# adaLN loads behind the boundary's weights, the time-step product in column groups, and decays from other queues, in a two-layer hybrid encoder on one core

## The chip, the core and the metric

One core of a Trainium2 chip runs the whole kernel. The metric is the device time of one execution in microseconds, lower is better, taken as the median of repeated runs. The engines are named as in the profile: PE is TensorE (matmuls), PEld its weight loads, DVE is VectorE, ACT is ScalarE, POOL is GpSimd and SP is SyncE, which only issues DMAs. ACT and POOL issue DMAs too. On chip data lie in SBUF (128 partitions); matmuls write to PSUM banks.

## The reference

One sequence of 512 tokens with 1024 features goes through two layers. The first mixes tokens with a gated short convolution, the second with a Mamba-2 state-space mixer; a SwiGLU feed-forward part follows each. Every part is wrapped in RMSNorms and in adaLN shift, scale and gate, which come from the conditioning vector `c`.

```python
mod = (jax.nn.silu(c) @ ada_w + ada_b).reshape(bsz, DEPTH, 2, 3, D_MODEL)
for i in range(DEPTH):
    shift, scale, gate = (mod[:, i, 0, k][:, None, :] for k in range(3))
    h = rmsnorm(x, norm_g[i, 0]) * (1.0 + scale) + shift
    y = short_conv_mixer(...) if i % 2 == 0 else ssd_mixer(...)
    x = x + gate * rmsnorm(y, norm_g[i, 1])
    shift, scale, gate = (mod[:, i, 1, k][:, None, :] for k in range(3))
    h = rmsnorm(x, norm_g[i, 2]) * (1.0 + scale) + shift
    y = swiglu_ffn(h, f_w_in[i], f_w_out[i])
    x = x + gate * rmsnorm(y, norm_g[i, 3])

def ssd_mixer(h, w_in, conv_w, conv_b, dt_bias, a_log, d_skip, norm_g, w_out):
    z, xbc, dt_raw = jnp.split(h @ w_in, [M_D_INNER, M_D_INNER + M_CONV_DIM], axis=-1)
    xbc = jax.nn.silu(causal_depthwise_conv(xbc, conv_w) + conv_b)
    xs, bm, cm = jnp.split(xbc, [M_D_INNER, M_D_INNER + g * n], axis=-1)
    dt = jax.nn.softplus(dt_raw + dt_bias)
    a = -jnp.exp(a_log)
    y = ssd_chunked(xs, dt, a, bm, cm) + d_skip * xs
    y = rms_normalize((y * jax.nn.silu(z)).reshape(..., groups)) * norm_g
    return y @ w_out
```

`ssd_chunked` sums `dt * a` along each chunk of 64 tokens (cs) and uses exp(cs) and differences of cs as decays. The columns of the state-space weight `m_w_in` are z (0 to 2047), xs (from `DIN` = 2048), B (from 2·`DIN`), C (from 2·`DIN`+`D`) and dt (32 columns from 6144).

## The kernel before

**Matmuls.** Activations lie feature-major, as `h[k]` tiles of 128 features by 512 tokens. Each float32 operand is split into a high part rounded to fp32r and a low part, and a product is three fp32r matmuls (high·high, high·low, low·high): `mm3`, which writes the lines L285, L286 and L287. One chunk of 128 output columns over K = 1024 is therefore 24 matmuls of 128x512. The split of a weight chunk (`split_w`, `load_w`) is a cast on ACT (L212 or L230) and a subtraction on DVE (L213 or L231).

**Order.** The programs of PE, ACT and DVE follow the order in which the code issues them in the blocks under `manual_schedule`; in the largest part of the kernel SP's and POOL's instructions are placed by a scheduler around that order. Each queue runs its instructions strictly one behind the other, so a waiting one holds up all that follow on that queue.

**Boundaries.** Between two parts stands a boundary: the last matmuls of one part, its norm and residual, the norm of the next part, the transposes of the result to feature-major (`tr`, xtr), the scale and shift (`u`), the split (`hi` on ACT, `lo` on DVE) and the first six weight chunks of the next part, the six leads (`k`, tile li). The table `BOUNDARY` in `out_begin` is that order, one step after the other; a step `name hf _ t` has a half of the tokens (0 or 1) and an index. The end of the table is

```python
hi1_2 hi1_3 lo1_2 k0_6 tr1_2 lo1_3 u1_4 hi1_4 u1_5 lo1_4 hi1_5 k0_7 tr1_3 lo1_5 u1_6 u1_7 hi1_6
hi1_7 lo1_6 k1_0 lo1_7 k1_1
```

The second half of tokens is finished in the leads only for K-tiles 0 and 1; tiles 2 to 7 (18 matmuls of 128x256 for each lead) follow as `rest(i)`. Hooks in `finish` run extra steps behind a named step.

**First boundary, into the first feed-forward part.** Its six leads come from `ffn_lead`; `after` loads the next weights (`more`, L221 on SP, two chunks, tile wst). adaLN's products for later parts run on DVE: rows of `ada_w` of 512 KB are loaded to staging tiles (`ada_load`, L1015, tile ada_st) and multiplied and added up (`ada_madd`, L127). `quarters` lists those still to be loaded. Each `ada_madd` frees a tile and issues the next load. Behind the boundary the feed-forward part computes sums of operand blocks and seven block products instead of eight (class `Units`: weights by `fetch`, with a sum that POOL's DMA adds up, L1241; class `Values`: sums of activations, L714 to L741; products sA, sB, sC, L665).

**Second boundary, into the state-space part.** `ssd_lead` lists the column ranges of the six leads: dt (32 columns padded with zeros to 128), two xs chunks, B, C, and the first z chunk of the first group of heads. The second z chunk is loaded by `load_w([(wm_in, P, P)])` as `more` and computed as a full chunk `pz` (`mm_chunk`, tile ip). The `u` values of the boundary lie in a rotating buffer of two.

**Opening of the state-space part.** `dt_steps` takes the raw dt (32 partitions, 512 tokens): transposes it to token-major (tokT, L1632), takes the softplus on DVE and ACT, builds the cumulative sums on PE (cumT, L1654), transposes them back (csh) and writes cs and exp(cs) to DRAM (cs_d, ecs_d, L1667 and L1669, from SP). `decays(g)` reads them back spread over all partitions (csb of 1 MB, two ecsb, L1677 and L1680, issued by ACT). `e_sub` (L1802), `e_exp` and `e_mul` turn csb into the decay matrices. `states` gives `prev`, which the product yo (L1825) reads. The convolutions of the four leads (`conv4`, tile cu) run between. `nxt` is the next group of heads; `nxt.weights(0)` loads its first weights (wst, L221) and `nxt.split(0)` casts the high part of the first chunk on ACT. `late_sums` continues adaLN's sums here (loads L1896); it also makes `four`, a 128x32 matrix on POOL that has a one in row p at column p mod 32.

## Time and profile before

| | us |
|---|---|
| median of 3 runs | 1322.79 (1322.65 to 1323.99) |
| profiled execution, its own time | 1323.32 |
| its span, first to last instruction | 1321.2 |
| PE busy | 1307.1 |
| DVE busy | 1023.3 |
| ACT busy | 724.7 |
| POOL busy | 109.9 |
| first boundary, its last steps and the start of the feed-forward part | about 223 to 265 |
| second boundary and opening of the state-space part | about 540 to 626 |

TensorE's mean granted clock is 0.998. All times inside the kernel are microseconds from the start of the span. In a row of the timeline the columns are start, duration, engine, line, operation, written tile<-read tiles, shapes and count; PE's matmuls are pipelined, so consecutive starts, not durations, give their cost. In a row of waits they are the waiting instruction, what it waited for, the total in us, how often, and the longest. "SPq" and "ACTq" rows are DMA issues.

### The profile page before, as it was taken

Reading aid. Unit: us, or ns where it says so; the run is one execution under the profiler, and the core shown is the slowest. Engines: PE = TensorE matmul, PEld = TensorE weight load, DVE = VectorE, ACT = ScalarE, POOL = GpSimd, SP = SyncE. Lnnn points to the kernel's source line nnn. Section 1 sums busy time; section 2 is a strip of 40 time slices with the busy share of each in tenths; the row PEclk is TensorE's granted clock in tenths of the full one; section 3 lists DMA queues with packets and bytes.
Section 4 is the critical chain, followed back from the end, with each engine's and each line's share of the span. In section 5 each row is a group of like instructions: output and inputs, shape, how many; then the busy total and the mean of one; then the engine's idle time right before and its main releaser. Section 6 shows DMA issues by size and latency. Waiting matters only on the chain.

```text
span 1321.2 us, 20459 instructions
## 1 busy us (share of the span) xinstructions
PE 1307.1 (99%) x7869; PEld 1149.2 (87%) x7869; DVE 1023.3 (77%) x1533; ACT 724.7 (55%) x1258; POOL 109.9 (8%) x135
## 2 busy tenths in 40 slices
PE   8999999999999999999999999999999999999998
PEld 7788889899998888898888888888789999998886
DVE  5577856978766987758998999977577777766888
ACT  5333345455533565656765667756574555544665
POOL 0000000111100240000000000000000111101330
PEclk9999999999999999999999999999999999999999
DMA  9767643789868983536764456523251888869871
GB/s 308 229 216 243 224 157 96 176 215 239 208 200 270 256 160 93 167 98 222 244 199 154 143 190 207 175 76 117 88 152 46 194 218 214 200 186 286 179 130 64
DMA packets 225429, 239.06 MB, mean 181 GB/s; under 512 B 10276, under 2 KB 177076, under 8 KB 224308
## 3 DMA queue, kind: packets, MB, share of 16 engines
q1 hardware_dynamic: 205008, 195.23, 47.7%
q0 software_dynamic: 16176, 29.63, 13.0%
q10 hardware_dynamic: 4148, 12.90, 3.0%
q8 instruction: 62, 1.02, 0.3%
q14 instruction: 35, 0.29, 0.1%
HBM read 203.76 MB, written 4.34 MB: 158 GB/s over the span
## 4 chain that ended last, share of the span: by engine, by line
PE 89%; DVE 4%; DMA 2%; ACT 2%; SPq 2%; issue 1%; DVEq 0%; ACTq 0%
PE sA L665 12%; PE ip L285 11%; PE ip L287 11%; PE ip L286 11%; PE y L387 8%; PE sC L665 6%; PE cA L2291 4%; PE sB L665 3%; PE cA L1322 3%; PE li L285 2%; PE li L287 2%; PE li L286 2%; PE li L947 1%; PE cD L2291 1%; PE cC L2291 1%; PE cB L2291 1%
## 5 line engine op out<-in xcount | busy, mean ns | idle before, releaser
L285 PE MATMUL ip<-h,whl 128*128 128x512 f32 x648 | 255.9, 395 | 0.2 <-DVE cv L1047 0.2
L287 PE MATMUL ip<-h,whl 128*128 128x512 f32 x648 | 252.4, 390 | 0.0
L286 PE MATMUL ip<-h,whl 128*128 128x512 f32 x648 | 252.3, 389 | 0.0
L285 PEld LDWEIGHTS ip<-h,whl 128*128 128x128 f32 x648 | 121.7, 188 | 26.2 <-issue 1.8
L287 PEld LDWEIGHTS ip<-h,whl 128*128 128x128 f32 x648 | 121.6, 188 | 25.8
L286 PEld LDWEIGHTS ip<-h,whl 128*128 128x128 f32 x648 | 121.8, 188 | 24.3
L665 PE MATMUL sA<-tq,whl 128*128 128x256 f32 x1008 | 131.2, 284 | 1.9 <-ACT g L675 1.9
L665 PEld LDWEIGHTS sA<-tq,whl 128*128 128x128 f32 x1008 | 125.8, 192 | 2.5 <-ACT g L675 2.1
L231 DVE TENSOR_TENSOR whl<-wst,whl 128x1024 fp32r<-128x1024 f32 x70 | 85.2, 1221 | 23.6 <-ACT whl L230 23.1
L127 DVE SCALAR_TENSOR_TENSOR ada_acc<-ada_st,csil,ada_acc 128x1024 f32<-128x1024 f32 x70 | 89.7, 1282 | 5.7 <-DMA ada_st<-in_ada_w_dram 4.3
L387 PE MATMUL y<-whlo,ys 128*128 128x512 f32 x384 | 89.6, 392 | 0.2 <-DVE ys L1936 0.2
L387 PEld LDWEIGHTS y<-whlo,ys 128*128 128x128 f32 x384 | 71.7, 188 | 16.4 <-issue 0.6
L285 PE MATMUL li<-h,whl 128*128 128x256 f32 x288 | 83.2, 289 | 0.0
L287 PE MATMUL li<-h,whl 128*128 128x256 f32 x288 | 81.5, 283 | 0.0
L286 PE MATMUL li<-h,whl 128*128 128x256 f32 x288 | 81.5, 283 | 0.0
L230 ACT CAST whl<-wst 128x1024 fp32r<-128x1024 f32 x70 | 72.7, 1040 | 2.2 <-DMA wst<-in_m_w_in_dram 2.2
L1241 POOL DMA_DIRECT2D sg<-sg x28 | 24.3, 870 | 535.5 <-DVE whl L213 230.0
L1690 DVE SCALAR_TENSOR_TENSOR cu<-ip,cols,cu 128x511 f32<-128x511 f32 (+2 forms) x84 | 62.8, 747 | 3.4 <-ACT cu L1687 1.4
L2291 PE MATMUL cA<-whlo,ao 128*128 128x512 f32 x264 | 61.0, 390 | 0.4 <-DVE c L2497 0.2
L2291 PEld LDWEIGHTS cA<-whlo,ao 128*128 128x128 f32 x264 | 49.3, 188 | 11.5 <-ACT whlo L2256 1.2
L285 PEld LDWEIGHTS li<-h,whl 128*128 128x128 f32 x288 | 55.2, 192 | 0.0
L286 PEld LDWEIGHTS li<-h,whl 128*128 128x128 f32 x288 | 55.2, 192 | 0.0
(383 smaller groups left out, 2680.7 us busy)
## 6 DMA issues: line engine op xcount, KB each, us to landing
ada_st<-in_ada_w_dram SPq DMA_DIRECT2D x96, 512.0 KB, 5.3
wsu<-in_f_w_in_dram SPq DMA_DIRECT2D x30, 512.0 KB, 5.8
sg<-in_f_w_in_dram SPq DMA_DIRECT2D x56, 256.0 KB, 3.4
wsu<-in_f_w_in_dram SPq DMA_DIRECT2D x56, 256.0 KB, 4.9
wst<-in_m_w_in_dram SPq DMA_DIRECT2D x14, 1024.0 KB, 5.3
wst<-in_f_w_in_dram SPq DMA_DIRECT2D x10, 1024.0 KB, 6.2
wst<-in_m_w_in_dram SPq DMA_DIRECT2D x20, 512.0 KB, 5.4
wst<-in_a_w_in_dram SPq DMA_DIRECT2D x9, 1024.0 KB, 7.1
```

The costliest lines, as they stand in the source:

```text
L127: dve.scalar_tensor_tensor(acc, w, csil[:, k:k + 1], acc, MUL, ADD)
L230: later.append((lambda sw=sw, w=w: act.copy(w[:, 0, :nk, :], sw), lambda sw=sw, w=w: dve.tensor_tensor(w[:, 1, :nk, :], sw, w[:, 0, :nk, : ...
L231: lambda sw=sw, w=w: dve.tensor_tensor(w[:, 1, :nk, :], sw, w[:, 0, :nk, :].bitcast(F32), SUB)))
L285: pe.matmul(dst, w_at(w, 0, kk), a[:, 0, sl], start=start, stop=False)
L286: pe.matmul(dst, w_at(w, 0, kk), a[:, 1, sl], start=False, stop=False)
L287: pe.matmul(dst, w_at(w, 1, kk), a[:, 0, sl], start=False, stop=stop)
L387: pe.matmul(pst, a[:, al, tk], wt[:, wl, kk, :], start=k == 0 and i == 0, stop=k == K - 1 and i == 2, skip_group_check=bool(held))
L665: pe.matmul(dst, w[:, wl, k0 + k, :], self.moving(q, k, al), skip_group_check=True, start=q in self.FIRST and k == 0 and i == 0, stop=k == ...
L1241: pool.dma_start(dst, src, accum_op=ADD)
L1322: pe.matmul(bank[r, sub], a[:, al, q, tk], w[:, wl, q, :], start=first and k == 0, stop=False, skip_group_check=True)
L1690: dve.scalar_tensor_tensor(u[:, sft:], pst[:, :T - sft], w[3 - sft], u[:, sft:], MUL, ADD)
L2291: pe.matmul(bank[r][sub], a[:, al, q, tk], w[:, hl, q, :], start=first and k == 0, stop=last and k == 2, skip_group_check=True)
```

## The change

It has four parts. The diff, cut to its core:

```diff
@@ first boundary @@
             madds = ada_begin(3)
+            put_off, quarters[:] = quarters[:], []
             begun = out_finish(parts, tail, ws0, {"lo0_7": (madds, madds), "lo1_3": (madds,)})
+            quarters[:] = put_off
...
             vs = Values(h, tq, va, [raw[1][:, 2 * b:2 * b + 2, :] for b in range(2)])
             lo_, hi_ = HALVES
+            for _ in range(3):
+                ada_load()
             part_of.fetch(0)
@@ second boundary @@
     ssd_lead = [lambda later, srcs=srcs: load_lead([(wm_in, c0, n) for c0, n in srcs], tile4l, later)
-                    for srcs in (((6144, NH), (DIN, P)), ((DIN + P, P), (2 * DIN, P)),
-                                 ((2 * DIN + D, P), (0, P)))]
+                    for srcs in (((DIN, P), (DIN + P, P)), ((2 * DIN, P), (2 * DIN + D, P)), ((0, P), (P, P)))]
...
             def u_(self, hi, j):
-                u = self.u[hi, j] = tmp.tile([P, 256], F32, tag="uh", name="u", bufs=2)
+                if values:
+                    u = self.u[hi, j] = values[j][:, HALVES[hi]]
+                else:
+                    u = self.u[hi, j] = tmp.tile([P, 256], F32, tag="uh", name="u", bufs=2)
...
-                               lambda: load_w([(wm_in, P, P)]), ys=ys, held=held)[2]
+                               lambda: None, ys=ys, held=held, values=values)[2]
...
-            begun = finish(tail_w, leads)
-        h, lead_ps, rest, wz1 = begun
+            va = wst_p.tile([P, 4, T], F32, tag="wst", name="va")
+            vb = [ao_p[0].tile([P, 2, T], F32, tag="ao", name="vb") for _ in range(2)]
+            values += [va[:, j, :] for j in range(4)] + [vb[j // 2][:, j % 2, :] for j in range(4)]
+            wdt = flat2(ao_p[0].tile([P, 2, T], F32, tag="ao", name="wdt"))[:, :KD * NH]
+            wdt = wdt.rearrange("p (k n) -> p k n", n=NH)
+            dma(wdt, wm_in[:, 6144:6144 + NH].rearrange("(k p) f -> p k f", p=P))
+
+            def dt_product():
+                pd = aux_ps("dtp")
+                for k in range(KD):
+                    g = k % 4 * NH
+                    pe.matmul(pd[g:g + NH, :], wdt[:, k, :], values[k], start=k < 4, stop=k >= 4,
+                              tile_position=(0, g), skip_group_check=True)
+                raw = t2("raw")
+                act.activation(raw, pd, AF.Identity, bias=dtb)
+                raws.append(raw)
+                yield
+
+            raws = []
+            begun = finish(tail_w, leads, {"lo1_7": (dt_product(),)})
+        h, lead_ps, rest, _ = begun
@@ dt_steps, decays @@
             for cc in range(NCH):
-                pe.transpose(pt[:, cc * NH:(cc + 1) * NH], raw[:, cc * P:(cc + 1) * P], ident[:NH, :NH])
+                pe.matmul(pt[:, cc * NH:(cc + 1) * NH], raw[:, cc * P:(cc + 1) * P], four[:, 0:NH],
+                          start=True, stop=True)
...
-            dma(cs_d.rearrange("h (c t) -> (h c) t", t=P), cs_hm)
+            dma_s(cs_d.rearrange("h (c t) -> (h c) t", t=P), cs_hm)
             act.activation(ecs_hm, cs_hm, AF.Exp)
-            dma(ecs_d.rearrange("h (c t) -> (h c) t", t=P), ecs_hm)
+            dma_s(ecs_d.rearrange("h (c t) -> (h c) t", t=P), ecs_hm)
...
-        def decays(g):
+        def decays(g, put=dma_s):
@@ opening @@
             nxt.weights(0)
...
-            convs = [cur.conv(i, lead_ps[1 + i]) for i in range(4)]
+            convs = [cur.conv(i, lead_ps[i]) for i in range(4)]
+            dts = dt_steps(raws[0])
+            next(dts)
             rest(0)
-            raw = dt_raw(lead_ps[0])
-            rest(1)
-            dts = dt_steps(raw)
-            next(dts)
             nxt.split(0)
...
-            rest(5)
             next(dts)
-            pz = mm_ps("ip")
-            mm_chunk(pz, wz1[0], h, ks=range(0, 2))
+            rest(4, range(2, 6))
             next(dts)
-            cur.e, cur.ecs = decays(0)
+            rest(4, range(6, KD))
+            cur.e, cur.ecs = decays(0, pool.dma_start)
...
-            mm_chunk(pz, wz1[0], h, ks=range(2, KD))
+            rest(5)
```

**adaLN's loads.** `quarters` is emptied while the first boundary is built, so no `ada_madd` in it issues the next load; three loads are issued after it, before `fetch(0)`. SP's queue, where ada_st are adaLN's loads, wst the weights `more` that follow the boundary's leads, and sg and wsu the first `fetch`. Before:

```order
L263 DMA wst<-in_f_w_in_dram 128x8x256
L1015 DMA ada_st<-in_ada_w_dram 128x1024 x6
L221 DMA wst<-in_f_w_in_dram 128x8x256
L604 DMA sg<-in_f_w_in_dram 128x4x128
L605 DMA sg<-in_f_w_in_dram 128x4x128
L608 DMA wsu<-in_f_w_in_dram 128x8x128
```

and now:

```order
L264 DMA wst<-in_f_w_in_dram 128x8x256
L1019 DMA ada_st<-in_ada_w_dram 128x1024 x3
L222 DMA wst<-in_f_w_in_dram 128x8x256
L1019 DMA ada_st<-in_ada_w_dram 128x1024 x3
L1652 DMA ea<-in_m_a_log_dram 128x32
L608 DMA sg<-in_f_w_in_dram 128x4x128
L609 DMA sg<-in_f_w_in_dram 128x4x128
L612 DMA wsu<-in_f_w_in_dram 128x8x128
```

Three of the six adaLN loads now stand behind the weights, and the small load of `m_a_log` (ea), which stood in the opening of the state-space part, stands here, ahead of the first fetch.

**dt.** The six leads are now the four convolution chunks and both z chunks. The padded lead, the memset of its pad, the separate load and split of the second z chunk and the chunk `pz` are gone. The boundary keeps its `u` values whole, in a weight buffer (va) and two others (vb). Behind step lo1_7, ahead of k1_1, eight float32 products of these values with the 32 dt columns (wdt) go into four column groups of one PSUM bank, two for each group. ACT adds the bias (dtb, now 128 rows, zero from row 32 on) and copies the four groups to raw (128x512); tokT is now a product with `four`, which adds up the groups and transposes at once. `four` is made earlier, after the first boundary, not in `late_sums`. The next group's first projection (`project(0)`) takes a bank of the other PSUM pool.

**The cast of the next group's weights.** The first cast of `nxt.split(0)` moves on ACT into the second boundary. There va and vb are the kept values, u before. Before:

```order
L522 CAST h_5076<-u 128x256
L519 ACTIVATE u<-xtr,mods,acol 128x256
L522 CAST h_5077<-u 128x256
L455 ACTIVATE ss<-ss 128x1
L519 ACTIVATE u<-xtr,mods,acol 128x256
```

and now:

```order
L526 CAST h_5081<-va 128x256
L523 ACTIVATE vb<-xtr,mods,acol 128x256
L231 CAST whl<-wst 128x1024
L526 CAST h_5082<-vb 128x256
L456 ACTIVATE ss<-ss 128x1
L523 ACTIVATE vb<-xtr,mods,acol 128x256
```

The cast (L231) stands between the value and the high part of feature tile 4. Its load (`nxt.weights(0)`) stands on SP behind wdt, two writes of x_d and one adaLN load; before, it was ahead of them all.

**The decays.** On ACT's queue in the opening, before:

```order
L1659 ACTIVATE dte_tok<-dte_tok 128x128
L1660 ACTIVATE dec<-cumT 128x128
L1668 ACTIVATE csb<-csb 128x128
L1677 DMA csb<-cs_d 128x2048
L1680 DMA ecsb<-ecs_d 64x2x512 x2
L1692 ACT_TABLE_LOAD
```

and now:

```order
L1683 ACTIVATE dte_tok<-dte_tok 128x128
L1684 ACTIVATE dec<-cumT 128x128
L1691 DMA cs_d<-csb 128x128
L1692 ACTIVATE csb<-csb 128x128
L1693 DMA ecs_d<-csb 128x128
L1716 ACT_TABLE_LOAD
```

The two writes come to ACT from SP, and the three reads of the first group go from ACT to POOL's queue; those of the later groups stay on ACT.

More of the change, by code (lines that the diff above doesn't have):

```diff
@@ L90, in trunk_kernel @@
     mcw = cols3
-    dtb = consts.tile([NH, 1], F32, name="dtb")
+    dtb = consts.tile([P, 1], F32, name="dtb")
+    pool.memset(dtb, 0.0)
     dcol = consts.tile([P, 16], F32, name="dcol")
@@ L372, in trunk_kernel, with out_begin @@
     LATE = 3
-    def out_begin(s, w, get_act, K, gg, xn_tile, first, lead, after, stage=None, ys=None, held=None):
+    def out_begin(s, w, get_act, K, gg, xn_tile, first, lead, after, stage=None, ys=None, held=None, values=()):
         ys = [None, None] if ys is None else ys
@@ L536, in k, with rest @@
                             kk == 0, kk == KD - 1)
-            def rest(self, i):
-                for kk in range(2, KD):
+            def rest(self, i, ks=range(2, KD)):
+                for kk in ks:
                     mm3(self.acc[i][:, HALVES[1]], self.ws[i], kk, self.h[kk], HALVES[1], False, kk == KD - 1)
@@ L1616, in st1 @@
             return sp.tile(list(shape), F32, name=name, tag=name, bufs=bufs)
-        def dt_raw(psd):
-            raw = t2("raw")[:NH, :]
-            act.activation(raw, psd[:NH, :], AF.Identity, bias=dtb)
-            return raw
         def dt_steps(raw):
@@ L1882, in norm @@
                     dve.scalar_tensor_tensor(y, y, mng[:, 2 * g + q:2 * g + q + 1], self.rg, MUL, MUL)
+        uh = tmp.tile([P, 256], F32, tag="uh", name="four", bufs=2)
+        four = uh[:, 0:P]
+        make_four(four)
         def late_sums():
-            uh = tmp.tile([P, 256], F32, tag="uh", name="four", bufs=2)
             sets, st = (64, 72, 80, 88), []
@@ L1900, in late_sums @@
                 load(n)
-            yield uh[:, 0:P]
+            yield
             for i, q0 in enumerate(sets):
@@ L1965, in trunk_kernel @@
             next(convs[0])
-            rest(2)
+            rest(1)
             next(convs[1])
@@ L1970, in trunk_kernel @@
             nxt.later[1][1]()
+            rest(2)
+            next(convs[2])
             rest(3)
-            next(convs[2])
-            rest(4)
             next(convs[3])
-            rest(5)
             next(dts)
-            pz = mm_ps("ip")
-            mm_chunk(pz, wz1[0], h, ks=range(0, 2))
+            rest(4, range(2, 6))
             next(dts)
-            cur.e, cur.ecs = decays(0)
+            rest(4, range(6, KD))
+            cur.e, cur.ecs = decays(0, pool.dma_start)
             for i in range(3):
@@ L1984, in trunk_kernel @@
             steps_late = late_sums()
-            four = next(steps_late)
-            make_four(four)
-            mm_chunk(pz, wz1[0], h, ks=range(2, KD))
+            next(steps_late)
+            rest(5)
             next(convs[3])
@@ L1990, in trunk_kernel @@
                 next(convs[i])
-            cur.project_z(0, lead_ps[5])
-            cur.project_z(1, pz)
+            for q in range(2):
+                cur.project_z(q, lead_ps[4 + q])
             nxt.later[2][0]()
```

15 lines of the change are left out of this document (9 added, 6 removed).

## The prediction

> **What bounds the kernel now.** I read the busy shares first, then what TensorE (PE) waits for, then the chain of waits at the two places that the change touches.
>
> ```profile
> PE 1307.1 (99%) x7869; PEld 1149.2 (87%) x7869; DVE 1023.3 (77%) x1533; ACT 724.7 (55%) x1258; POOL 109.9 (8%) x135
> PE sA L665 <- ACT g L675: 1.9, 1, 1.9
> PE sC L665 <- DVE raw L1209: 0.2, 1, 0.2
> ```
>
> PE is busy in 1307.1 of 1321.2 us, and its longest wait once the loads have begun to come is 1.9 us. So the kernel is a queue of matmuls without holes. Only two things shorten it: fewer matmuls, or one of these small waits gone. Work taken from ScalarE (ACT), VectorE (DVE) or a DMA queue counts only if a PE wait hangs on it. Where 1.9 us comes from, the chain shows (start, us, what):
>
> ```profile
> 223.50 7.27 DMA wst<-in_f_w_in_dram
> 230.79 1.06 ACT whl L212
> 231.87 2.37 DVE whl L213 x2
> 237.94 1.29 DVE ada_acc L127
> 259.56 0.28 ACT g L675
> 259.88 2.15 PE sA L665 x12
> ```
>
> It starts at a weight load that lands late, and 36 us of DVE and ACT work run behind it almost without a gap to the matmul that waits.
>
> **Part 1, the adaLN loads held back.** SyncE's queue (SP) and ACT at that place (on the ACT rows, the idle time before them in brackets):
>
> ```profile
> 181.94 41.51 SPq L1015 DMA_DIRECT2D ada_st<-in_ada_w_dram  x5
> 223.50 0.43 SPq L221 DMA_DIRECT2D wst<-in_f_w_in_dram  x1
> 225.11 0.38 SPq L604 DMA_DIRECT2D sg<-in_f_w_in_dram  x1
> 225.77 0.86 ACT L522 CAST h<-u 128x256 fp32r<-128x256 f32 x2 [1.26 <-DVE u L517]
> 230.79 2.00 ACT L212 CAST whl<-wst 128x1024 fp32r<-128x1024 f32 x2 [4.16 <-DMA wst<-in_f_w_in_dram]
> sg<-in_f_w_in_dram SPq DMA_DIRECT2D x56, 256.0 KB, 3.4
> ```
>
> The load of wst stands behind adaLN loads that each wait until DVE has used a staging buffer, so it is issued at 223.50. In the changed order three of those loads come behind it, and it can go out at about 189, when the three ahead of it have been issued. Then ACT casts as soon as its own work ends, at 226.63 (225.77 + 0.86), not at 230.79: the head of the chain starts 4.16 us earlier. PE needs 1.9 + 0.2 us of that (the waits at sA and sC), so 2.1 is the most; PE itself cannot run ahead. I take **-2.0**. The ends are 0 (another input becomes the last) and -2.1. What is late next: the first fetch (sg, then the accumulating DMA on POOL). The load of m_a_log now stands ahead of it on SP and waits for the boundary's last DVE step, so sg goes out some 2.4 us after 225.11, at about 227.5. With 3.4 us to landing (the median of the sg loads) that is 231, and what is read from it, the sum on POOL and then split_y, comes only after the DVE steps on the values. The three held-back loads then feed the first sums(2), which is at 237.94 in the old chain; their data are of 512 KB and are issued before the wsu. If they land last, DVE stops there and the gain goes: that is a rival below.
>
> **Part 2, dt.** Removed: one chunk of 24 matmuls 128x512 (pz, the second z chunk, now among the six leads in place of the padded dt lead). Two rows of PE 24 matmuls apart give its price:
>
> ```profile
> 599.02 0.39 PE L285 MATMUL ip<-h,whl 128*128 128x512 f32 x1
> 604.46 0.39 PE L285 MATMUL ip<-h,whl 128*128 128x512 f32 x1
> 18.76 0.39 PE L947 MATMUL li<-h,whl_b 128*128 128x512 f32 x1
> 19.08 1.08 PE L194 MATMUL ada_pe<-ada_st,rows 128*32 128x128 f32 x32
> 20.09 0.96 PE L947 MATMUL li<-h,whl_b 128*128 128x512 f32 x3
> 926.01 1.10 PE L1868 MATMUL ssg<-accg,ones 128*128 128x512 f32 x2
> ```
>
> 604.46 - 599.02 = 5.44 us, or 0.227 each: **-5.44**. Added: dtp, eight float32 products of 32 columns over 512, k-th into column group k mod 4. The kernel has the same form already, with 128 columns in motion: ada_pe, 16 products shown as 32 passes, in 1.08 us. From 18.76 to 20.09 is 1.33, less 0.23 for the li matmul itself leaves 1.10, and the three li behind it take 0.96 where three pipelined ones take 0.39 + 2 x 0.23 = 0.85: in all about 1.2 us. One float32 pass of 512 costs about 0.45 by ssg (two passes in 1.10, less the 0.17 by which a 0.39 matmul outlasts its pitch), so one of 128 about 0.11; 32 of them in a row would be 3.6. Hence four run at once: eight slots, 0.87, and 0.35 for going into the tiled form and out. For dtp: 16 passes, four at once, 4 x 0.45 = 1.8, plus 0.35 is 2.15; with 0.43 a pass and the switch half hidden it is 1.9. I take **+2.0**. All in a row it would be 16 x 0.45 = 7.2, the other bound.
>
> tokT goes from transposes to float32 products, eight passes for four. The rows, with the pitch of the 128x256 matmuls ahead of it:
>
> ```profile
> 583.55 0.28 PE L286 MATMUL li<-h,whl 128*128 128x256 f32 x1
> 583.67 0.28 PE L287 MATMUL li<-h,whl 128*128 128x256 f32 x1
> 583.88 0.43 PE L1632 MATMUL tokT<-ident,raw 32*128 32x32 f32 x4
> 584.24 0.39 PE L285 MATMUL li<-h,whl 128*128 128x256 f32 x1
> 592.97 0.39 PE L1654 MATMUL cumT<-ea,mask 128*128 128x128 f32 x2
> ```
>
> Four passes take 0.36 (584.24 - 583.88), so four more are **+0.3** (0.1 to 0.4). Part 2 is -5.44 + 2.0 + 0.3 = **-3.1** (-3.5 to -2.6). The memset, the load and the split of one weight chunk that also go (a CAST of 1.0, a subtraction of 1.2) lie on ACT and DVE under running matmuls: nothing. The memset of dtb adds 0.1 at the start on POOL, and PE's first matmul needs only what stands ahead of it: nothing, at most 0.1.
>
> Does the dt chain still arrive? Its end on DVE:
>
> ```profile
> 591.68 0.29 DVE L1650 SCALAR_TENSOR_TENSOR ea<-dt_tok,ea 128x128 f32<-128x128 f32 x1
> ```
>
> It ends at 591.97 with ea, and cumT on PE, which reads it, follows 1.0 later at 592.97. In the changed order tokT has 36 matmuls of 128x256 (two of the six rest passes, 36 x 0.12 = 4.3 us) less ahead of it and dtp more: 2.3 earlier, at 581.6. cumT too loses 36 and gains dtp and the longer tokT: 2.0 earlier, at 591.0. The slack stays at about 1 us; nothing is added. dtp's own inputs are there: the last value is written by DVE just ahead of the last 18 matmuls, as before, and wdt (128 KB) is loaded ahead of the adaLN load of 552.44 (below), over 20 us before.
>
> **Part 3, the decays.** On the queues now:
>
> ```profile
> 595.43 0.34 SPq L1667 DMA_DIRECT2D cs_d<-csb  x1
> 598.74 0.36 ACTq L1677 DMA_DIRECT2D csb<-cs_d  x1
> 600.58 1.28 ACT L1692 ACT_TABLE_LOAD   x1 [4.84 <-DVE cu L1690]
> 607.48 2.46 ACT L1802 ACTIVATE csb<-csb,cs_tok 128x128 f32<-128x128 f32 x8
> DMA to landing us min/median/max: 5.0/6.3/7.5
> 620.46 0.42 DVE L1793 TENSOR_TENSOR prev<-prev,st 128x256 f32<-128x256 f32 x1
> 624.24 1.50 PE L1825 MATMUL yo<-ct,prev 128*128 128x128 f32 x12
> ```
>
> The two writes take 0.8 us of ACT's queue, inside its 4.84 us of idling. The csb load (1 MB), which waits 3.3 us for the write, goes out 2.0 us earlier, like cumT, at 596.7, now on POOL, and e_sub(0) wants it at about 604.4 (607.48 less part 2's 3.1). Issued like POOL's other transfers (0.86 us a piece) and landing as the csb loads did (5.0 to 7.5 after the issue), it is there at 602.6 to 605.1: 0 to 0.7 us of waiting on ACT. PE notices only through prev, which ends 3.4 us before yo (624.24 - 620.88): nothing, up to 3.4 us of lateness.
>
> By the Trainium skill, "DMA: Bandwidth & Descriptors", SWDGE vs HWDGE, the queue of POOL builds its descriptors in SBUF state from which a busy DVE can lock it out, which speaks against this move; DVE is busy in those 10 us. The page's own fit for such a transfer, 2.0 us plus the bytes at 436 GB/s, makes 4.4 us of 1 MB, an estimate by which nothing is late.
>
> **Part 4, a cast that moves.** At the second boundary the high part of the next group's weights now stands in ACT's order between u0_4 and hi0_4, and its load on SP stands behind x_d and an adaLN load:
>
> ```profile
> 552.44 1.34 SPq L1896 DMA_DIRECT2D ada_st<-in_ada_w_dram  x2
> 558.71 0.56 ACT L519 ACTIVATE u<-xtr,mods,acol 128x256 f32<-128x256 f32 x1
> 564.25 1.34 ACT L499 ACTIVATE xn<-x,ss 128x512 f32<-128x512 f32 x2
> 566.95 0.60 PE L508 MATMUL xtr<-ident,xn 128*128 128x128 f32 x4
> wst<-in_m_w_in_dram SPq DMA_DIRECT2D x14, 1024.0 KB, 5.3
> ```
>
> Issued at about 552.8 and 5.3 us on the way (the median), it lands at 558.1, before ACT gets there at 559.3. Everything behind it on ACT (hi0_4, the squares, the root, xn) is then 1.0 later; xn ends at 566.6 at worst, not 565.59, and PE's transpose of it is at 566.95: hidden, with 0.4 left. It costs from a landing after 559.7 on, us for us; I count 0 (to +1).
>
> **Sum.** -2.0 - 3.1 = -5.1 against the profiled execution: its span of 1321.2 plus the 2.1 around it are 1323.3, which becomes 1318.2. The median of the runs lies 0.5 below the profiled one (1322.8 for 1323.3), so I say **1317.7**; its own range is 1316.4 to 1319.3.
>
> **Rivals.**
> (a) *The gain at the first boundary only moves.* Another input is last there: the held-back adaLN loads at sums(2), or sg. For it: DVE runs without a gap from 231.87 on, so any late input is passed on. Against: these loads are out before 231. Then part 2 remains: -3.1, 1319.7. 11%.
> (b) *The column groups do not overlap at 512 columns.* Then dtp is 7.2 + 0.35, part 2 is +2.4, the whole +0.4: 1323.2. Only the ada_pe row, with 128 columns, speaks against it. 6%.
> (c) *Slower: the csb load drags on POOL's queue.* If that queue moves bytes in proportion to its 256 KB sums, which land after 4.8 us in the median,
>
> ```profile
> DMA to landing us min/median/max: 3.3/4.8/10.8
> ```
>
> 1 MB takes 19.2 us from the end of its issue (597.6) and lands at 616.8; wanted at 604.4, it is 12.4 late, and 3.4 of that is hidden ahead of yo: +9.0, less 5.1, is +3.9: 1326.7. It decides from a landing after 607.8 on, and makes the kernel slower by more than 0.2% from 615.6 on. Against: those sums also read their target back and take an engine's addition, and the DMA engines are the same for all queues. 8%.
> (d) *The cast blocks the second boundary.* A landing of 7 us or more, x_d and two adaLN loads being in flight: PE waits 1 to 2 at xtr: 1319.2. 5%.
>
> **How the numbers follow.** Forecast 70%, (a) 11, (b) 6, (c) 8, (d) 5. The range 1315.8 to 1320.8 takes in the forecast's own range with the runs' spread of 0.6 below, (a) and (d), and leaves out (b) and (c), some 16%, with a little at the lower end. 0.2%, 2.65 us, is about what can be told from no change: faster means under 1320.1. Faster: 69 of the forecast's 70, 8 of (a), 4 of (d): 81%. Within: (b), the rest of (a) and (d) and 1: 11%. Slower: (c), 8%.
>
> **What would show it.** Right: PE's list of waits without sA from g; wst issued near 189; 16 passes of dtp in about 2 us; 24 fewer L285 to L287 rows of 128x512; no PE wait for xtr above 0.5 us at the second boundary; csb landed within 8 us of POOL's issue and no PE wait at yo. Wrong: DVE idle for ada_st behind the fours of the first boundary (a), dtp of 7 us (b), ACT idle before e_sub(0) above 3.4 us (c), ACT idle before the moved cast (d). A gain above 5.6 would mean that something ran earlier which I do not see.

## The result, and the profile after

The changed kernel takes 1317.76 us (median of 6, 1316.24 to 1319.07) against 1323.04 us before (median of 6); the ratio is 0.9958, 95% interval [0.9945, 0.9971]. That is 5.3 us faster, 5.1 was forecast, and 1317.7 as the time. Its profiled execution has a span of 1316.1 us. One execution, in experiment 12, took 1432.84 us at a granted clock of 0.85; the ratios leave it out, and the median given there, 1316.79, is 1316.69 without it. The sum came out right with terms off in opposite directions, so that it fits this closely is in part luck, and most of what follows is about those terms.

Busy shares and PE's longer waits after the change, behind the start of the kernel (waiting instruction, what for, us in total, times, longest):

```profile
PE 1301.8 (99%) x7865; PEld 1142.9 (87%) x7865; DVE 1020.2 (78%) x1531; ACT 723.4 (55%) x1257; POOL 113.2 (9%) x139
PE xtr L509 <- ACT xn L500: 1.1, 3, 0.6
PE ggp L320 <- DVE gcol L159: 0.8, 1, 0.8
PE yo L1851 <- DVE prev L1819: 0.2, 1, 0.2
```

PE is busy 5.3 us less, and sA from g is gone from the list. The wait at ggp lies in the convolution layer, where nothing was changed; a second profile of the same kernel (below) does not have it. The spans of its six executions lie between 1314.0 and 1316.1 us, so steps are read here as the shift of single matmuls between neighbouring places, not as differences of spans.

At the first boundary, SP and ACT after the change:

```profile
182.62 5.87 SPq L1019 DMA_DIRECT2D ada_st<-in_ada_w_dram  x2
188.54 0.43 SPq L222 DMA_DIRECT2D wst<-in_f_w_in_dram  x1
217.16 6.96 SPq L1019 DMA_DIRECT2D ada_st<-in_ada_w_dram  x3
228.17 0.43 SPq L608 DMA_DIRECT2D sg<-in_f_w_in_dram  x1
227.21 1.99 ACT L213 CAST whl<-wst 128x1024 fp32r<-128x1024 f32 x2
```

The weights go out at 188.5 (189 was said), ACT casts them without waiting, and sg goes out at 228.2; neither PE nor DVE waits for it.

In the opening of the state-space part, dtp and tokT on PE with the matmuls around them, and the first decays on POOL and ACT:

```profile
573.91 0.28 PE L288 MATMUL li<-h,whl 128*128 128x256 f32 x1
574.12 1.06 PE L1614 MATMUL dtp<-va,wdt 128*32 128x512 f32 x8
575.01 1.04 PE L1614 MATMUL dtp<-vb,wdt 128*32 128x512 f32 x8
575.98 0.39 PE L286 MATMUL li<-h,whl 128*128 128x256 f32 x1
578.23 0.98 PE L1655 MATMUL tokT<-four,raw 128*128 128x32 f32 x8
579.04 0.36 PE L286 MATMUL li<-h,whl 128*128 128x256 f32 x1
```

```profile
594.12 0.56 POOL L1701 DMA_DIRECT2D csb<-cs_d  x1 [109.44 <-DVE cu L1714]
603.96 2.45 ACT L1828 ACTIVATE csb<-csb,cs_tok 128x128 f32<-128x128 f32 x8 [3.02 <-DMA csb<-cs_d]
```

From the last li before dtp to the first behind it are 2.07 us; one pitch of 0.12 is that matmul's own, so dtp costs 1.95, and 0.1 more shows at the next li. tokT takes 0.81, before 0.36. The csb read lands 9.8 us after its issue, and ACT stands 3.0 us for it.

At the second boundary, the moved cast on ACT and, on PE, the four transposes that follow it by way of xn, with the first li behind them:

```profile
556.91 1.05 ACT L231 CAST whl<-wst 128x1024 fp32r<-128x1024 f32 x1 [1.20 <-DMA wst<-in_m_w_in_dram]
563.39 0.87 PE L509 MATMUL xtr<-ident,xn 128*128 128x128 f32 x4
564.02 0.36 PE L286 MATMUL li<-h,whl 128*128 128x256 f32 x1
```

The weights of the cast went out at 549.65 and landed after 7.2 us, where 5.3 was taken. ACT stood 1.2 us for them, xn came later by that and the cast, and the transposes with the step to the next li take 0.63 us, 0.35 before (566.95 to 567.30). These 0.3 us are not among PE's waits: the one that waits is PEld, for the weights of a transpose (PEld for xn, 0.3).

The next table gives the starts of six matmuls in us, the shift against the kernel before in brackets. Rows: sC just ahead of the wait at the first boundary, the first full sA product behind it, the first li behind a transpose of the second boundary, the first xtok of the opening, the first yd of the second group of heads, the first transpose of the third boundary. "Again" is a second profile of the changed kernel, "reads on ACT" an experiment below.

| matmul | before | after | again | reads on ACT |
|---|---|---|---|---|
| sC | 254.93 | 255.28 (+0.35) | 254.27 (-0.66) | 254.23 (-0.70) |
| sA | 264.35 | 261.04 (-3.31) | 260.03 (-4.32) | 259.99 (-4.36) |
| li | 567.30 | 564.02 (-3.28) | 563.68 (-3.62) | 563.09 (-4.21) |
| xtok | 609.90 | 603.54 (-6.36) | 603.19 (-6.71) | 602.59 (-7.31) |
| yd | 665.68 | 659.97 (-5.71) | 659.94 (-5.74) | 658.36 (-7.32) |
| xtr | 975.17 | 969.91 (-5.26) | 969.18 (-5.99) | 967.60 (-7.57) |

So the first boundary gives 3.66 us in both profiles (0.35 + 3.31, 4.32 - 0.66). Counted from the product ahead of sC, so that the wait at sC is in it as in the forecast's 2.0, it is 3.99 in both (sA starts at 253.17 before, 253.85 and 252.84 after): twice the forecast. The opening from li to xtok gives 3.08 and 3.09; 3.1 was forecast. Between xtok and the second group's yd 0.65 and 0.97 are lost again; nothing was forecast there.

### The profile page after: what moved, and what is told of

Same layout as the page of the kernel before. It is cut to its first block, busy times and chain, and to the rows that moved or that the text cites. A ratio compares the mean times of both kernels' runs of the same rounds, so it can differ in the third digit from the quotient of the medians.

```text
span 1316.1 us, 20444 instructions
## 1 busy us (share of the span) xinstructions
PE 1301.8 (99%) x7865; PEld 1142.9 (87%) x7865; DVE 1020.2 (78%) x1531; ACT 723.4 (55%) x1257; POOL 113.2 (9%) x139
## 4 chain that ended last, share of the span: by engine, by line
PE 83%; DVE 7%; DMA 4%; ACT 3%; SPq 2%; issue 1%; ACTq 0%; DVEq 0%; POOLq 0%
PE sA L669 12%; PE y L388 8%; PE ip L286 8%; PE ip L288 8%; PE ip L287 8%; PE sC L669 6%; PE cA L2316 4%; PE cA L1327 3%; PE sB L669 3%; PE li L286 2%; PE li L288 2%; PE li L287 2%; DMA ada_st<-in_ada_w_dram 2%; PE li L951 1%; DVE ada_acc L128 1%
## 5 line engine op out<-in xcount | busy, mean ns | idle before, releaser
L286 PE MATMUL ip<-h,whl 128*128 128x512 f32 x640 | 252.6, 395 | 0.2 <-DVE cv L1051 0.2
L288 PE MATMUL ip<-h,whl 128*128 128x512 f32 x640 | 249.3, 390 | 0.0
L287 PE MATMUL ip<-h,whl 128*128 128x512 f32 x640 | 249.2, 389 | 0.0
L286 PEld LDWEIGHTS ip<-h,whl 128*128 128x128 f32 x640 | 120.2, 188 | 25.8 <-issue 1.8
L288 PEld LDWEIGHTS ip<-h,whl 128*128 128x128 f32 x640 | 120.1, 188 | 25.5
L287 PEld LDWEIGHTS ip<-h,whl 128*128 128x128 f32 x640 | 120.2, 188 | 24.0
L231 ACT CAST whl<-wst 128x1024 fp32r<-128x1024 f32 x70 | 72.7, 1040 | 1.8 <-DMA wst<-in_m_w_in_dram 1.8
L286 PEld LDWEIGHTS li<-h,whl 128*128 128x128 f32 x288 | 55.2, 192 | 0.8 <-issue 0.8
L287 PEld LDWEIGHTS li<-h,whl 128*128 128x128 f32 x288 | 55.2, 192 | 0.0
L288 PEld LDWEIGHTS li<-h,whl 128*128 128x128 f32 x288 | 55.1, 191 | 0.0
```

Source lines behind the costliest of these rows:

```text
L231: later.append((lambda sw=sw, w=w: act.copy(w[:, 0, :nk, :], sw), lambda sw=sw, w=w: dve.tensor_tensor(w[:, 1, :nk, :], sw, w[:, 0, :nk, : ...
L286: pe.matmul(dst, w_at(w, 0, kk), a[:, 0, sl], start=start, stop=False)
L287: pe.matmul(dst, w_at(w, 0, kk), a[:, 1, sl], start=False, stop=False)
L288: pe.matmul(dst, w_at(w, 1, kk), a[:, 0, sl], start=False, stop=stop)
```

## Experiments

All times of a group were taken beside the kernel before on the same chip: 1322.84 for experiments 1, 2, 3 and 5, 1322.58 for 6 to 9, 1322.85 for 4, 10, 11 and 12.

**1. The hold-back alone.** The kernel before with

```diff
+            put_off, quarters[:] = quarters[:], []
             begun = out_finish(parts, tail, ws0, {"lo0_7": (madds, madds), "lo1_3": (madds,)})
+            quarters[:] = put_off
...
+            for _ in range(3):
+                ada_load()
             part_of.fetch(0)
```

> The kernel before with part 1 alone (adaLN's loads held back). The prediction's theory: only the waits at sA and sC go, 2.0 us: about 1321.0 against 1323.0. The theory formed from the trace of after: the wait of 1.9 us in the kernel before is followed by some 16 matmuls at a pitch of 0.21 instead of 0.12 us, with a granted clock of 0.72 to 0.86 in that stretch; the clock falls because PE stood, so removing the wait is worth 2.1 + 1.5 = 3.6 us: about 1319.4. By the one PE's clock in the stretch behind the boundary stays below 0.9, by the other it is 1.00.

1319.18 us, ratio 0.9973 [0.9962, 0.9983]: 3.7 us faster. The stretches behind the boundary, of the kernel before (first two rows) and of this one. Columns: the stretch, its length, busy us of PE, PEld, DVE, ACT and POOL with instructions, the granted clock, DMA share, GB/s.

```profile
258.00:262.00 4.00, 2.15 (x14) 2.12 (x14) 3.94 (x6) 3.06 (x6) 0.99 (x2) 0.86 0.89 252
262.00:266.00 4.00, 4.00 (x26) 3.86 (x25) 3.46 (x6) 1.49 (x3) 0.76 (x1) 0.72 1.00 213
```

```profile
258.00:262.00 4.00, 3.94 (x33) 3.74 (x33) 3.45 (x6) 1.62 (x3) 0.63 (x1) 1.00 0.96 191
262.00:266.00 4.00, 4.00 (x35) 4.00 (x35) 3.69 (x6) 2.74 (x6) 0.00 (x0) 1.00 0.49 144
```

In the kernel before PE is busy for all of 262 to 266 and yet starts 26 matmuls there instead of 35: the clock granted is 0.72. The wait of 1.9 us is followed by matmuls at about half speed. With the load early both are gone. The second theory holds for the size and for the clock; what the slow stretch is worth by itself, experiments 3 and 4 ask.

**2. Everything but the hold-back.** The changed kernel with those lines undone.

> The changed kernel with part 1 undone; dt and decays as changed. Prediction's theory: 2.0 us slower than the changed kernel, 3.1 faster than before: about 1319.9. Theory with the slow clock: 3.6 slower than the changed kernel, about 1321.3, that is 1.7 faster than before, if the dt part is worth 3.1 less about 1 us that the trace of after shows lost behind it (waits at xtr, yo and yd); with nothing lost behind it 1319.9 too. The row of waits shows sA from g again in both, and the pitch of 0.21 behind it only if the clock theory holds.

1320.09 us, ratio 0.9982 [0.9974, 0.9991]: 2.8 faster than before, where the changed kernel is 5.3 faster. The wait is back, and the slow stretch with it:

```profile
PE sA L669 <- ACT g L679: 1.9, 1, 1.9
```

```profile
258.00:262.00 4.00, 2.73 (x14) 2.73 (x15) 4.00 (x8) 2.44 (x5) 1.75 (x2) 0.70 0.94 261
```

The time lies between the two that were named, its interval (1319.4 to 1321.7) holds both, and it does not tell them apart; the windows do. The 3.7 of experiment 1 and the 2.8 here are more than the 5.3 of both together; the intervals allow that, and in this profile only 0.2 is lost between xtok and yd (shifts of -4.01 and -3.82), where the changed kernel loses 0.65 and 0.97.

**3. Keeping PE at work in the wait, first try.** The kernel before with

```diff
+                if u == 0:
+                    for _ in range(16):
+                        pe.matmul(un.banks["B", 0][:, HALVES[1]], un.wts["X", 0][:, 0, 4, :], h[4][:, 0, HALVES[0]],
+                                  start=True, stop=True, skip_group_check=True)
                 un.product(u, "P6")
```

> The kernel before with 16 matmuls of 128x256 put into PE's order just ahead of the product that waits at the first boundary (P6 of the first unit); nothing reads their result. They fill 16 x 0.12 = 1.9 us, the length of the wait, so the wait itself is not shortened. If the slow matmuls behind the wait come from PE having stood (clock), they go back to 0.12 and the time falls by 1.3 to 1.5 us, to about 1321.6. If they come from late operands or weight loads, the pitch stays 0.21 and the time is that of before (1323.0), or longer by what the 16 overlap badly (up to 0.3).

1328.08 us, ratio 1.0042 [1.0030, 1.0055]: 5.2 slower, which neither theory said. The bank was a bad choice: its other half is still read by DVE, the added matmuls waited for that, and PE stood longer than before.

```profile
PE sB L1434 <- DVE g L679: 4.6, 1, 4.6
```

```profile
258.00:262.00 4.00, 0.00 (x0) 0.00 (x0) 4.00 (x8) 2.49 (x5) 0.89 (x2) 0.89 0.65 191
262.00:266.00 4.00, 3.89 (x18) 3.89 (x19) 2.48 (x4) 0.02 (x1) 0.86 (x1) 0.50 1.03 220
```

It did not answer its question, but it shows the effect again: behind the longer wait the clock is 0.50, and 18 matmuls fit where 35 do at full clock.

**4. The same with a bank of its own.**

```diff
+                if u == 0:
+                    pw = aux_ps("warm")
+                    for _ in range(16):
+                        pe.matmul(pw[:, HALVES[0]], un.wts["X", 0][:, 0, 4, :], h[4][:, 0, HALVES[0]],
+                                  start=True, stop=True, skip_group_check=True)
                 un.product(u, "P6")
```

> The kernel before with 16 matmuls of 128x256 ahead of the product that waits at the first boundary, now into a PSUM bank of their own that nothing reads. They fill 1.9 us of the 2.1 us for which PE stood. Clock theory: the 16 or so matmuls behind go from a pitch of 0.21 back to 0.12, the granted clock there to 1.00, and the kernel is 1.4 to 1.6 us faster than before, about 1321.2, though more work is done. Operand theory (the slow pitch is lateness of weights or values): the pitch stays 0.21 and the time is that of before.

1322.69 us, ratio 1.0001 [0.9993, 1.0010]: no change. PE in its profiled execution, of which only the stretch up to 266 is read (it took 1326.79 in all, above the median: at the third boundary PE waits 2.2 us for xn and a slow stretch follows, which the kernel before does not have). The kernel before comes first:

```profile
259.88 2.15 PE L665 MATMUL sA<-tq,whl 128*128 128x256 f32 x12 [1.85 <-ACT g L675]
261.83 2.68 PE L665 MATMUL sC<-h,wss 128*128 128x256 f32 x12
264.35 1.59 PE L665 MATMUL sA<-h,whl 128*128 128x256 f32 x12
```

```profile
257.62 2.08 PE L1435 MATMUL warm<-h,whl 128*128 128x256 f32 x16
259.63 1.70 PE L665 MATMUL sA<-tq,whl 128*128 128x256 f32 x12
261.17 1.60 PE L665 MATMUL sC<-h,wss 128*128 128x256 f32 x12
262.61 1.60 PE L665 MATMUL sA<-h,whl 128*128 128x256 f32 x12
265.63 1.10 PE L665 MATMUL sA<-tq,whl 128*128 128x256 f32 x7 [1.42 <-ACT g L675]
```

The clock theory is right about the cause of the slow matmuls. Those behind the filled wait keep the 0.12 pitch (sA to sC 1.54, before 1.95; sC to sA 1.44, before 2.52), with the same weights and operands. It is wrong about what that is worth: PE is 1.74 earlier at 262.61, and then stands 1.4 us for ACT at the next product, which starts at 265.63, only 0.25 before the 265.88 of the kernel before. So the chain on DVE and ACT that begins with the late weights is late for two products. PE's lateness of 3.7 us was set by that chain as much as by the clock; in the kernel before PE spent it as one wait and a slow stretch, here as fill and a second wait. Only an earlier chain takes it away, which is what the hold-back does.

**5. The dt products one behind the other.** The changed kernel with

```diff
-                    g = k % 4 * NH
-                    pe.matmul(pd[g:g + NH, :], wdt[:, k, :], values[k], start=k < 4, stop=k >= 4,
-                              tile_position=(0, g), skip_group_check=True)
+                    pe.matmul(pd[:NH, :], wdt[:, k, :], values[k], start=k == 0, stop=k == KD - 1)
...
-                act.activation(raw, pd, AF.Identity, bias=dtb)
+                act.activation(raw[:NH, :], pd[:NH, :], AF.Identity, bias=dtb[:NH])
```

and tokT over 32 rows of raw and `four`.

> The changed kernel with the eight dt products in one column group, one behind the other, instead of four groups side by side. If the four groups run side by side (dtp 1.9 us in the trace of after), the serial form takes 16 passes of 0.43 to 0.45 = 6.9 to 7.2 us: 5 us slower than the changed kernel, about 1322.8. Rival: the dt products overlap with other things whatever their form, or the passes of 32 columns are cheaper: less than 2 us slower, under 1319.8.

1322.17 us, ratio 0.9997 [0.9988, 1.0006], against 0.9958 with the column groups: of the gain of 5.3 us 0.7 are left. Its dtp on PE:

```profile
573.20 3.62 PE L1613 MATMUL dtp<-va,wdt 128*32 128x512 f32 x8
576.66 3.60 PE L1613 MATMUL dtp<-vb,wdt 128*32 128x512 f32 x8
```

Eight passes in 3.46 us (576.66 - 573.20) are 0.43 each, where the column groups take 0.89 for eight (575.01 - 574.12). Four do run side by side at 512 columns. Without them the dt part would have cost time: li starts at 563.10 and xtok at 608.05, so the shift goes from -4.20 to -1.85, a loss of 2.35, where rival (b) priced +2.4.

**6. The changed kernel again.**

> The changed kernel itself, unchanged, as the mark for the next three: about 1317.8 (5.3 faster than before). Its trace says whether the extra waits of the first profile (ggp 0.8, xtr of the second boundary 1.1 in all, yo 0.2 and the half microseconds at yd and at the third boundary) are there every time. If they belong to the change, they come again; if they are scatter, the span is about 1 us shorter without them.

1317.82 us, ratio 0.9961 [0.9949, 0.9974], span 1315.0. The waits at ggp and the larger ones at xtr did not come again, one of 0.4 at cA did that the first profile does not have; the loss between xtok and yd came again (the table's column "again"). That loss belongs to the change.

**7. The moved cast put back behind the boundary.** The changed kernel with

```diff
-            nxt.split(0)
             next(dts)
+            nxt.split(0)
             next(convs[0])
```

> The changed kernel with one line moved: the split of the next group's weights behind the second step of the dt chain, so that its first cast leaves the second boundary's ACT order. Prediction's theory: the cast lies hidden, same time as the changed kernel within 0.3 us. Theory from the trace of after: ACT stood 1.2 us for the load of those weights and PE's wait for xtr rose from 0.6 to 1.1: 0.5 us faster than the changed kernel. Rival: the cast, now behind ea and its table load, and the subtraction on DVE delay the dt chain: up to 1 us slower.

1317.38 us, ratio 0.9959 [0.9946, 0.9971], not to be told from 1317.82. PE's listed wait for xn at the second boundary is 0.3 in the kernel before, in both profiles of the changed one and here, so the rest of the 1.1 in the first profile's list lay at other boundaries. But the cast was not quite hidden where it stood: the transposes with the step to li take 0.35 us here as before the change, 0.63 and 0.65 in the changed kernel. Behind the boundary the cast makes the dt chain late instead:

```profile
PE cumT L1678 <- DVE ea L1674: 1.2, 1, 1.2
```

**8 and 9. The decays' reads from ACT's queue, and from SP's.** The changed kernel with one argument changed:

```diff
-            cur.e, cur.ecs = decays(0, pool.dma_start)
+            cur.e, cur.ecs = decays(0)
```

or `decays(0, dma)` for SP.

> The changed kernel with the first group's decay reads back on ACT's queue; the writes stay on ACT. In the trace of after the csb read lands 9.8 us after POOL issued it and ACT waits 3.0 us for it, with 0.2 us of it reaching PE. Theory that POOL's queue is the slow one: csb lands 6 to 7 us after an issue at about 594, the wait on ACT falls under 1 us; the time is that of the changed kernel or 0.2 less, as ACT's queue stands about 2 us for the write first. Theory that the DMA engines are full there whatever the queue: landing again 9 to 10 us after the issue and the time 0 to 1 us longer, for ACT has lost its 2 us.

> The same with the three reads on SP's queue, behind two adaLN loads and ahead of the next weights. If POOL's queue is the slow one: landing 5 to 7.5 us after an issue at about 594, wait on ACT under 1 us, 0.2 us faster than the changed kernel. If the engines are full: landing 9 to 10 us, no change; and the next weights are later by 2 to 3 us behind the waiting reads on SP, which the slack of those casts hides.

From ACT 1316.15 us, ratio 0.9950 [0.9938, 0.9963]; from SP 1316.65, ratio 0.9952 [0.9938, 0.9966]; beside them POOL with 1317.82. Issue of the read and start of e_sub(0), from ACT:

```profile
592.63 0.33 ACTq L1701 DMA_DIRECT2D csb<-cs_d  x1
602.07 2.45 ACT L1828 ACTIVATE csb<-csb,cs_tok 128x128 f32<-128x128 f32 x8 [0.67 <-DMA csb<-cs_d]
```

and from SP:

```profile
592.73 0.82 SPq L1925 DMA_DIRECT2D ada_st<-in_ada_w_dram  x2
593.64 0.38 SPq L1701 DMA_DIRECT2D csb<-cs_d  x1
602.69 2.45 ACT L1828 ACTIVATE csb<-csb,cs_tok 128x128 f32<-128x128 f32 x8 [1.84 <-DMA csb<-cs_d]
```

The read takes 9 to 10 us from each queue (9.4 from ACT, 9.0 from SP, 9.8 from POOL), so the lateness does not come from POOL's queue alone. By the Trainium skill, "DMA: Bandwidth & Descriptors", Issuing engines are not separate DMA queues, transfers of all queues end up on the same 16 DMA engines, with which these three landings agree; experiments 11 and 12 show what difference between the queues is left. The issue differs too: 3.3 us after the issue of the cs_d write from ACT (589.32 there), 3.5 from SP, 3.9 from POOL (590.27 to 594.12 in the changed kernel). Both theories were half right. The gain was larger than either said, since e_sub, e_exp and prev of the first group, 2 to 3 us late on ACT, leave the second group's ACT work late too: in the changed kernel its yo waits for prev, with the reads on ACT the list has no wait of PE from 600 to 665. From the second group's first yo to its first yd it is 1.91 and 1.93 us in the two profiles of the changed kernel, 1.43 with the reads on ACT (656.93 to 658.36); that is 0.5 of the 0.65 and 0.97, and where the rest goes is open. In the changed kernel:

```profile
658.06 0.60 PE L1851 MATMUL yo<-ct,prev 128*128 128x128 f32 x4
658.88 1.16 PE L1851 MATMUL yo<-ct,prev 128*128 128x128 f32 x8 [0.21 <-DVE prev L1819]
```

**10. All of part 3 undone.** Writes from SP, reads from ACT.

> The changed kernel with all of part 3 undone: writes from SP's queue, reads on ACT's. If ACT's writes bring nothing, the time is that of the kernel with the reads on ACT (1316.2, 6.4 faster than before); if SP's queue holds the writes up behind a weight load or the adaLN loads, csb lands 1 us or more later than there and the time is 0.5 to 1 us longer.

1321.36 us, ratio 0.9986 [0.9977, 0.9994], with runs from 1318.4 to 1323.1: 1.5 us faster than before, where the changed kernel gains 4.8 to 5.3 and the one with writes and reads on ACT 6.4. The profiled execution is the slowest of them, at 1323.06. SP's queue in it, a wait on it, and ACT's:

```profile
594.25 0.34 SPq L1925 DMA_DIRECT2D ada_st<-in_ada_w_dram  x1
594.64 0.42 SPq L1691 DMA_DIRECT2D cs_d<-csb  x1
```

```profile
SPq L1925 <- PE li L288: 4.4, 1, 4.4
```

```profile
598.47 0.36 ACTq L1701 DMA_DIRECT2D csb<-cs_d  x1
601.33 1.28 ACT L1716 ACT_TABLE_LOAD   x1 [9.31 <-DVE cu L1714]
```

```profile
PE cb L1796 <- DVE cu L1714: 2.6, 1, 2.6
```

The cs that the write takes was there at 591.7, but an adaLN load ahead of it on SP waited for a matmul to free its tile, and the write went out at 594.6. The reads then held ACT's queue, the convolutions' silus behind them came late, and PE stood 2.6 us, with a granted clock of 0.71 from 608 to 612. In the changed order the writes had to leave SP; the forecast priced that move at nothing either way.

**11 and 12. The two adaLN loads ahead of the read held back too.** In `late_sums`, with the reads on POOL, and on ACT:

```diff
-            for n in range(6):
+            for n in range(4):
                 load(n)
             yield
+            for n in range(4, 6):
+                load(n, dma_s)
```

where `load` takes the queue as an argument.

> The changed kernel, reads on POOL as in it, but the two adaLN loads (512 KB each) that go out 1.3 us ahead of the csb read are issued by ACT behind e_sub(0). If the 9 to 10 us to landing, seen from all three queues, come from the DMA engines being full with those loads, csb lands 3 us sooner (6 to 7 us after its issue), ACT's wait of 3.0 to 3.3 us falls below 0.7, yo waits no more, and the time is 1.0 to 1.6 us below the changed kernel's: about 1316.5. If POOL's queue itself is slow, the landing stays at 9 us or more and the time at 1317.8.

> Both: reads on ACT and the two adaLN loads held back to behind e_sub(0). The candidate for the best version. The reads on ACT alone left no wait at yo, so the earlier landing should bring nothing more: the time of that kernel, 6.4 us faster than before, about 1316.2 (within 0.4); 0.4 faster than that if ACT's 0.7 us wait for csb still reached PE somewhere.

With POOL 1317.30 us, ratio 0.9957 [0.9945, 0.9968]; with ACT 1316.79, ratio 0.9952 [0.9939, 0.9965]. With POOL:

```profile
594.24 0.56 POOL L1701 DMA_DIRECT2D csb<-cs_d  x1 [108.66 <-DMA ecs_d<-csb]
601.65 2.47 ACT L1828 ACTIVATE csb<-csb,cs_tok 128x128 f32<-128x128 f32 x8 [0.50 <-DMA csb<-cs_d]
```

The landing falls from 9.8 to 7.4 us with POOL's queue unchanged, ACT's wait from 3.0 to 0.5, and nothing is lost from xtok to yd (-6.16 and -6.18). With the reads on ACT it falls further, from 9.4 to 5.0; POOL first, then ACT (size, us from issue to landing):

```profile
csb<-cs_d POOLq DMA_DIRECT2D x1, 1024.0 KB, 7.4
csb<-cs_d ACTq DMA_DIRECT2D x1, 1024.0 KB, 5.0
```

So two things made the read late: the 1 MB of adaLN loads issued just ahead of it, worth 2.4 us of landing on POOL and 4.4 on ACT, and POOL's queue, worth 2.4 where those loads are out of the way (one profile each). How far ahead the loads go matters too: on POOL 9.8 with the first of them 1.3 us ahead and 8.2 with 2.4 (experiment 7). It is not the whole account, for in experiment 10, on ACT, the read took 8.8 with the first load 4.2 us ahead. The kernel before, whose csb reads all go out on ACT, has this over those of the eight whose landing its profile gives:

```profile
DMA to landing us min/median/max: 4.7/7.3/11.0
```

The times do not show what the hold-back is worth: with POOL the ratio is 0.9957, and 0.9958 and 0.9961 without it. With the reads on ACT nothing more is gained, as expected.

The best version by its median is the changed kernel with the first reads on ACT's queue: 1316.15 us, 6.4 faster than before. Its five runs beside those of the changed kernel on the same chip are 1315.4 to 1316.8 against 1316.6 to 1318.4; the trace accounts for 0.7 to 1.0 of the 1.7 between the medians, and the rest may be scatter.

## Why the prediction was right, point by point

- **What bounds the kernel:** right. PE is the queue that everything is paid in, and the time followed the shifts on PE.
- **Part 1, -2.0:** the mechanism was right, load, queue and chain as described, the size was not: 3.7, or 4.0 with the wait at sC. The step that failed is "PE needs 1.9 + 0.2 us of that (the waits at sA and sC), so 2.1 is the most". Only waits were counted. Behind a wait of 1.9 us PE ran slow, which no list of waits shows, and the chain on DVE and ACT was late for the next product as well: with the slow stretch filled away, a second wait of 1.4 us stood in its place (experiment 4). The row was quoted in the prediction: 12 matmuls of sA in 2.15 us where 12 at a pitch of 0.12 take 1.6.
- **Part 2, -3.1:** right at 3.08, and its terms too: dtp 2.05 for 2.0, tokT 0.45 more for 0.3. Four column groups at once (experiment 5).
- **Part 3, nothing:** wrong by +0.65 to +0.97 for the reads on POOL. The landing of 5.0 to 7.5 us was that of two reads of the kernel before, the first of which, with the two adaLN loads 2.4 us ahead of it, took the 7.5. Over more of that kernel's reads it is 4.7 to 11.0 (experiments 11 and 12), so the 9.8 and 10.0 that came lie within what that kernel shows. The loads are 1.3 us ahead now, and the queue is another; both count. The slack of 3.4 us ahead of yo held in the first group (prev ends at 616.40, yo starts at 617.86), but the step ended there: that ACT stays late into the second group was not followed. Moving the writes was not free of effect either: left on SP, with the reads on ACT, they leave 1.5 us of the gain (experiment 10).
- **Part 4, nothing:** nearly right, 0.3 us. The landing of 5.3 us was the median of these loads; this one took 7.2, ACT stood 1.2 for it, and what the prediction counted as hidden with 0.4 left came 0.3 late at xtr. The price that it gave, us for us from a landing after 559.7 on, fits roughly: 556.9 with PE 3.3 us earlier is 560.2, 0.5 past that.
- **Rivals:** (a) did not happen. (b) is excluded by experiment 5. (c) happened in its first half, a late csb, at a fraction of its price: 9.8 to 10.0 us to landing and not 20.1 (596.7 to 616.8), in part for the reason named, POOL's queue, and in part for the adaLN loads ahead. The condition of (d), a landing of 7 us or more, was met with 7.2, and its sign, ACT idle before the moved cast, is there; its price of 1 to 2 us was 0.3.

So -5.1 was right as a sum with 1.7 too little counted at the first boundary and 0.65 to 0.97 of loss not counted in the opening, besides 0.3 for the cast. From sC to the second group's yd the shift of PE is -6.1 in one profile and -5.1 in the other (-5.71 - 0.35, -5.74 + 0.66); the ratio's interval is 3.8 to 7.3 us, so the runs hold both that and the forecast.

## What to carry to other kernels

A wait of PE of some 2 us can be worth more than its length when it is removed, here 3.7 us for 1.9, because the matmuls behind it run slow and that is no wait: compare the number of matmuls in equal stretches, or the granted clock, behind each such wait. The slow stretch can hide a second wait, so making it fast by filling the wait with work does not help where the chain that was waited for is late for the next consumer too. A wait can also sit on the weight load of a matmul and be missing from PE's list; the step from one matmul to the next shows it. When loads are reordered, look for what is issued just ahead of each urgent transfer and on any queue, take a landing time from all transfers of that kind and not from the nearest two, and follow a late result one round further than its first consumer.

## What the runs showed of the hardware that was not expected

- Inside the kernel, waits of PE between 1.9 and 4.6 us were each followed by some microseconds at half pace: 0.213 us from one 128x256 matmul to the next instead of 0.120, for 3.4 us behind the wait of 1.9 and 5.7 behind that of 4.6, and 0.427 for 128x512 instead of 0.227 (experiment 10). After the waits of 1.4 us in experiment 4 and 1.2 us in experiment 7 the pitch was 0.12 again within three matmuls. The Trainium skill, "TensorE: Matmul & The Clock Gate", Part 1: The HAM clock gate, has the two speeds, but lets the clock fall after an idle window of about 3.4 us; here 1.9 us were enough, and the measurement decides.
- The slow stretch need not begin at once: in the kernel before, the first eight matmuls behind the wait still ran at 0.12; in experiment 2 it began with the fourth.
- Float32 matmuls on four column groups at 512 columns run four at a time: 0.89 us for eight passes, 3.46 in one group.
- A broadcast read of 1 MB from DRAM took 5.0 us from ACT's queue and 7.4 from POOL's with the adaLN loads held back (experiments 12 and 11), and 9.0 to 10.0 from ACT, SP or POOL with 1 MB of them issued 0.8 to 1.4 us ahead.
